# Where the big SBUF tiles begin: slots of 4096 bytes on multiples of 2 KB in a transformer block on one Trainium2 core

## The chip, the cores and the metric

The kernel runs on 1 core of one Trainium2 chip. The metric is the device time of one execution in microseconds (us), the median of several runs. A kernel's instructions stand in five queues, one for each engine: TensorE (PE; its weight loads are listed as PEld), VectorE (DVE), ScalarE (ACT), GpSimd (POOL) and SyncE (SP), which issues the DMAs.

## The reference

One transformer block on 1024 tokens of width 1024, in float32. Four mixers (banded attention, a gated recurrence, spatial gating, a gated linear recurrence) share one projection `h @ w_in`, their outputs are merged through gates, and a SwiGLU network follows:

```python
for l in range(DEPTH):                       # one layer
    h = rms_norm(x, norm_mix_pre[l])
    y = hybrid_mixer(h, w_in[l], ...)        # sum over 4 branches of sigmoid(gates) * (o_n @ w_branch), then @ w_out
    x = x + rms_norm(y, norm_mix_post[l])
    h = rms_norm(x, norm_ffn_pre[l])
    x = x + rms_norm(swiglu(h, w_ffn_in[l], w_ffn_out[l]), norm_ffn_post[l])

# of the gated linear recurrence, the causal convolution over four tokens
xp = jnp.pad(xin, ((0, 0), (CONV_W - 1, 0), (0, 0)))
xc = conv_b + xp[:, 0:S] * conv_w[0]
for j in range(1, CONV_W):
    xc = xc + xp[:, j:j + S] * conv_w[j]
```

## The kernel before, in words

**Precision.** Every float32 operand of a large product is split in two float32r parts, a high one (`split`, L133, a copy on ACT) and a low one (L134, a subtraction on DVE). A product is then three matmuls for each K tile: `mm3` (L205 to L210) multiplies high by high, high by low and low by high. Of the arguments of `nc.tensor.matmul` the one called `lhsT` is the stationary operand (128 x 128 values, loaded ahead) and the one called `rhs` is the moving operand, which is read from SBUF column by column while the matmul runs. With 512 float32 columns the moving operand is 2048 bytes long in each partition.

**Where operands lie.** SBUF is cut by pools. `slot` (L78) gives one of 33 big tiles of the pool "slots". Activations, their sums and most intermediate results lie in slots: the transposed activations `hTh`, `hTl`, `h2h`, `h2l` (two K tiles of 512 tokens in one slot), the sums `T1` to `T4`, the branches' outputs `oh`, `ol`, the fetched `back`. The pool "ring" holds the raw weight blocks (`raw`, L146) and their split parts (`whi`, `wlo`, L155 and L156). `wtmp`, `tmp` and `mtmp` give 2 KB temporaries and smaller ones from two further pools.

```python
    SW = 1028
    def slot(name, dt=F32, w=D):
        cnt[0] += 1
        t = sp.tile([P, SW], dt, tag="S", name=f"{name}_{cnt[0]}", bufs=NSLOT)
        return t[:, :w]
```

A slot is 1028 floats, 4112 bytes, and slots stand 4128 bytes apart. In the program as it is built, slot k begins at byte 27616 + 4128 k of its partition, for k = 0 to 32. Counted from a multiple of 2048, the starts are 992, 1024, 1056 and so on up to 2016: none is a multiple of 2 KB, all are multiples of 32, and every 512-column operand that lies in a slot runs across a multiple of 2 KB. The ring begins at byte 163840, which is 80 x 2048, and every one of its tiles begins on a multiple of 2 KB. The 2 KB temporaries begin 1152 bytes past one.

**Which products read which.** In the Winograd products `wino` (L320 to L357), the gates, the branch projections and the plain part of the SwiGLU input, the weights in the ring are stationary and the activations in the slots move, 512 columns at a time. In the token-major products `gemm_tm` (L224) the weights move, 256 columns at a time. In the product with `w_ffn_out` (`ffn_out`, L1168 to L1309, matmuls L1226 to L1228) both operands are split into one tile, and its second half moves, 512 columns: a ring tile as a rule, but in the last of three calls, which goes bank by bank over three pairs of K tiles (so 3 x 4 x 3 = 36 matmuls for a product), the second, fourth, sixth and seventh product take slots for it (`spare`, L1214 and L1246), since the ring alone would not hold them.

**The order.** Instructions of each engine stand in the order that the tile framework's scheduler gives, from the program's order and its priorities. The stages are: first norm and transposes; projections by Winograd, results kept in DRAM; gates ahead of time, Winograd as well; the recurrences, filled up with plain gate products; attention and spatial gating beside the gated merge; output projection and second norm; SwiGLU input by Winograd; SwiGLU output, norm, residual and store.

**The convolution.** `fetch_d` (L736) fetches the input of the linear recurrence into a slot from column 4 on, and POOL zeroes columns 0 to 3 (L738). `rglru` then reads four shifted views of 1024 columns (L747 and L749):

```python
        nc.vector.tensor_scalar(xc, X[:, 1 : S + 1], cw(0), col(C_CB + j), op0=ALU.mult, op1=ALU.add)
        for t in range(1, 4):
            nc.vector.scalar_tensor_tensor(xc, X[:, 1 + t : S + 1 + t], cw(t), xc, op0=ALU.mult, op1=ALU.add)
```

Of the kernel before, what the change touches and what calls it, by code (L numbers as in the profile page):

```python
# [17 lines left out]
P = 128  # L18
# [13 lines left out]
# columns of the packed per-partition vectors  # L32
C_GMIX, C_GFFN, C_LB, C_HG, C_GM, C_CW, C_CB, C_BA, C_BX, C_LAM = 0, 8, 16, 18, 20, 22, 30, 32, 34, 36
NCOLS = 38


@with_exitstack
def hybrid_trunk(ctx, tc, x, w_in, w_branch, w_out, w_ffn_in, w_ffn_out, cols, gpost, gfpost,
# [7 lines left out]
    cp = pool("const", 1)  # L46
    sp = pool("slots", 1)
    rp = pool("ring", 2)
    sm = pool("small", 4)
# [5 lines left out]
    def enter(name, bufs):  # L55
        """pool that gives its place to the next one"""
        if scope:
            scope.pop("s").close()
        scope["s"] = ExitStack()
        scope["p"] = scope["s"].enter_context(tc.tile_pool(name=name, bufs=bufs))  # L60
# [10 lines left out]
    # quarters of a plain gate product after each step of the recurrences, to fill the tensor engine's waits  # L71
# [3 lines left out]
    SW = 1028  # L75
    cnt = [0]

    def slot(name, dt=F32, w=D):  # L78
        cnt[0] += 1
        t = sp.tile([P, SW], dt, tag="S", name=f"{name}_{cnt[0]}", bufs=NSLOT)  # L80
        return t[:, :w]
# [44 lines left out]
    def after(ins):  # L126
        """in the program order of its engine after ins"""
        return tc.issue_after(ins.ins) if ins is not None else nullcontext()

# [20 lines left out]
    def wunit(name, src):  # L150
        """split one 4 KB unit of a raw block; src: AP of [P, a, b]"""
        cnt[0] += 1
        shp = list(src.shape)
        with tc.high_priority(AHEAD_SPLIT if started else 0):
            hi = rp.tile(shp, F32R, tag="whi", name=f"whi_{name}_{cnt[0]}", bufs=NRING)  # L155
            lo = rp.tile(shp, F32R, tag="wlo", name=f"wlo_{name}_{cnt[0]}", bufs=NRING)  # L156
            split(src, hi, lo)
        return hi, lo

    def interleave(back, front, n_back=1, n_front=1):  # L160
        """emit the two streams in turns; the longer one ends alone"""
        live = [[iter(back), n_back], [iter(front), n_front]]
        while live:
            for it in list(live):
                for _ in range(it[1]):
                    try:
                        next(it[0])
                    except StopIteration:
                        live.remove(it)
                        break  # L170

    def zipped(*streams):
        """one step of each stream in turn"""
        live = [iter(st) for st in streams]
        while live:
            for it in list(live):
                try:
                    yield next(it)
                except StopIteration:
                    live.remove(it)  # L180

    def filled(fill, stream, counts):
        """counts[i] steps of fill after the i-th step of the stream"""
        for i, _ in enumerate(stream):
            drive(take(fill, counts[i] if i < len(counts) else 0))
# [19 lines left out]
    def mm3(ps, lh, ll, rh, rl, n, more=False, ks=None):  # L205
        """accumulate over n contraction tiles; lh(k) etc. give APs; more: onto a finished group's sum"""
# [31 lines left out]
    def rstd_of(ss, n, w):  # L238
        """(ss / n + eps) ** -0.5 on [P, w]"""
        ms = small("ms", w)  # L240
        nc.gpsimd.tensor_scalar(ms, ss, 1.0 / n, EPS, op0=ALU.mult, op1=ALU.add)
        r = small("rstd", w)
        last[2] = nc.gpsimd.tensor_tensor(r, ms, neghalf[:, :w], op=ALU.pow)
        return r
# [4 lines left out]
    def halves(name):  # L249
        """token halves: slot [P, 2 k, 512] for each half and pair of k"""  # L250
# [13 lines left out]
    # Winograd's form of Strassen's product: quadrants of (columns x K) of the weights, of (K x tokens) of the  # L264
    # activations z. B_ij: K half i, token half j
    # T1 = B12 - B11, T2 = B22 - T1, T3 = B22 - B12 = T2 - B11, T4 = T2 - B21
# [40 lines left out]
    def column_sums(c0_, c1_):  # L307
        """S1 = A21 + A22, S2 = S1 - A11, S3 = A11 - A21, S4 = A12 - S2, in the order of the blocks"""
# [11 lines left out]
    def wino(ops, c0_, c1_, done):  # L320
        """two column tiles c0_, c1_ ([P, KT, P]) as the column halves of one Winograd step;
        done(column tile, token half, source, tile to use) takes the quadrants"""
# [37 lines left out]
    def normed(xtile, wait=None):  # L360
        """rms-normalised (without gain) [128 tokens, D]"""
# [8 lines left out]
    def place_T(srcs, tt, gcol, Th, Tl):  # L370
        """transpose token tiles tt, tt + 1, apply the gain per channel, split"""
# [29 lines left out]
    def twice_silu(dst, ps):  # L401
        """x * (1 + tanh(x / 2)) = 2 silu(x)"""
# [4 lines left out]
    def twice_gelu(dst, ps):  # L407
        """x * (1 + tanh(c (x + a x^3))) = 2 gelu(x)"""
# [22 lines left out]
    def fetch(key, j, w=D):  # L431
        t = slot(f"{key}{j}", w=w)
        nc.sync.dma_start(t[:, w - S :], stage[key, j])
        return t
# [3 lines left out]
    def proj_cm(key, fn, c=None):  # L438
        """fn(column tile, source, result)"""
# [17 lines left out]
    def proj_tm(key, fn):  # L457
        """token-major result, two times [P, 4 tiles, 256]"""
# [21 lines left out]
    # ======================= mixer B: gated recurrence =====================  # L480
# [27 lines left out]
    def hgrn(j):  # L508
# [5 lines left out]
        # s = t: sum over a head's channels of q k, placed on the diagonal of every tile  # L514
# [15 lines left out]
        def level(l):  # L530
            """scores of s in an even block of 2^l tokens with t in the odd block that follows"""
            # the two heads' products in turns: they lie in different row groups of the array
# [12 lines left out]
            # only the odd blocks' columns, and no rows past the last even block  # L545
# [32 lines left out]
        # state at the start of every 128-token tile  # L578
# [60 lines left out]
    # ======================= mixer A: banded attention =====================  # L639
# [93 lines left out]
    # ======================= mixer D: gated linear recurrence ==============  # L733
    Dm = {"O": [None, None]}

    def fetch_d(j):  # L736
        Dm[j] = [fetch("dx", j, w=SW), fetch("dg", j)]
        nc.gpsimd.memset(Dm[j][0][:, 0:4], 0.0)  # L738

    def rglru(j):  # L740
# [6 lines left out]
        nc.vector.tensor_scalar(xc, X[:, 1 : S + 1], cw(0), col(C_CB + j), op0=ALU.mult, op1=ALU.add)  # L747
        for t in range(1, 4):
            nc.vector.scalar_tensor_tensor(xc, X[:, 1 + t : S + 1 + t], cw(t), xc, op0=ALU.mult, op1=ALU.add)  # L749
# [12 lines left out]
        # w / 2 = 4 r softplus(-lam), a = exp(-w) = (1 - th) / (1 + th)  # L762
# [4 lines left out]
        # sqrt(1 - a^2) = 2 sqrt(th) / (1 + th)  # L767
# [15 lines left out]
    # ======================= mixer C: spatial gating =======================  # L783
# [37 lines left out]
    # ======================= gated branch merge ============================  # L821
# [5 lines left out]
    def gates_pre(items):  # L827
        """gate columns ahead of their branch: tanh kept in DRAM"""
# [68 lines left out]
    def gates_last(n, o):  # L897
        """the last branch, with the split of the result: first token half first"""
# [22 lines left out]
    # ======================= order of the mixing block =====================  # L921
# [9 lines left out]
    with tc.issue_after(last[0].ins), tc.issue_after(last[1].ins), tc.issue_after(last[2].ins):  # L931
# [24 lines left out]
        _sv = [0]  # L956

        def sv(w=2):
            _sv[0] += 1
            return cp.tile([P, w], F32, name=f"sv{_sv[0]}")  # L960

        # forget-gate lower bound: cumsum(softmax over depth) - p[0], one layer
# [13 lines left out]
        # 2 * softplus(-lam), softplus(z) = max(z, 0) + log1p(exp(-|z|))  # L976
# [26 lines left out]
    # the quadrant that no product needs waits in DRAM  # L1003
# [50 lines left out]
    # ======================= output projection, residual, second norm ======  # L1054
# [55 lines left out]
    # ======================= SwiGLU ========================================  # L1110
# [11 lines left out]
    def ffn_plain(g):  # L1122
        """hidden tiles 2 g, 2 g + 1 by direct products"""
# [18 lines left out]
        # starts on the token half that is ready first  # L1142
# [7 lines left out]
    def ffn_wino(f, rg, ru):  # L1150
        """gate and up columns of hidden tile f: the two column halves of one Winograd step"""
# [14 lines left out]
    # the same for the product of the activations with w_ffn_out: f tiles in pairs (a K half each),  # L1166
    # quadrants of (tokens x K) and of (K x columns), four PSUM banks for the 512 tokens of a product
    def ffn_out(chunk, first, final):  # L1168
# [63 lines left out]
        def prod(pst, A, B, evac, more=False, after=None):  # L1232
            """onto the four banks pst; more: onto the sum they hold"""
# [11 lines left out]
            # bank by bank  # L1245
# [20 lines left out]
        def half_done(tt, c_, second):  # L1266
            """sum of squares of a column half, then its gain; with the second half norm, residual and store"""
# [23 lines left out]
        def into_last(r, c_, second):  # L1291
            """the last product that adds to this quadrant"""
# [93 lines left out]
```

## Time and profile before

| what | value |
|---|---|
| median of 3 runs | 1629.66 us (1629.09 to 1633.43) |
| the profiled execution: span from first to last instruction | 1631.2 us |
| PE busy | 1555.7 us, 95% of the span, 7880 matmuls |
| DVE, ACT, POOL busy | 1061.5, 571.4 and 607.1 us |
| mean granted TensorE clock | 0.987 of full speed |
| DMA | 191.48 MB, mean 117 GB/s |

The page gives of the profiled execution its span alone; this lies 1.5 us above the median and within the three runs' range, so a change that is worked out from the trace is put onto the median as it stands. Matmuls are pipelined: a matmul's own duration (some 395 ns for 512 columns) spans its way through the array and overlaps the next one, so what a matmul costs is the distance from one start to the next. A window of the trace counts every matmul that reaches into it.

### The profile page before, as it was taken

How to read it: one execution, taken by the hardware profiler on the slowest of the kernel's cores; microseconds unless marked ns; L12 is line 12 of the kernel's file. 1: busy time of each engine (PE TensorE's matmuls, PEld its weight loads, DVE VectorE, ACT ScalarE, POOL GpSimd, SP SyncE). 2: the span in 40 equal slices, each digit the busy share in tenths (PEclk: the TensorE clock that was granted, in tenths of full speed). 3: DMA queues.
4: the chain of work that ended last, by engine and by line, in shares of the span. 5: the costliest groups of instructions: out<-in, count | busy, mean ns of one | idle time of the engine just before them, and what ended most of it. 6: DMA issues, size and time to landing. Idle time of an engine off the chain costs nothing. (4 is left out here: it accounts for less than half of the span.)

```text
span 1631.2 us, 20634 instructions
## 1 busy us (share of the span) xinstructions
PE 1555.7 (95%) x7880; PEld 1276.4 (78%) x7880; DVE 1061.5 (65%) x1415; ACT 571.4 (35%) x945; POOL 607.1 (37%) x477
## 2 busy tenths in 40 slices
PE   7899999999998999999999987999999999898986
PEld 7888888888887877676889966888888888686865
DVE  5985664434469475666765698555555556869898
ACT  6333332333321253324335533222222223353533
POOL 2674333322100200222332256433333334829195
PEclk9999999999999999999999998999999999999998
DMA  6234333333461148432325411222222235530212
GB/s 239 93 101 158 104 110 103 104 110 104 150 224 49 56 155 297 181 142 75 120 91 181 169 58 65 84 78 78 84 78 78 78 111 218 205 105 14 90 51 105
DMA packets 108547, 191.48 MB, mean 117 GB/s; under 512 B 6432, under 2 KB 65440, under 8 KB 108448
## 3 DMA queue, kind: packets, MB, share of 16 engines
q1 hardware_dynamic: 108448, 190.16, 33.7%
q8 instruction: 62, 1.02, 0.3%
q14 instruction: 37, 0.30, 0.1%
HBM read 136.66 MB, written 53.48 MB: 117 GB/s over the span
## 5 line engine op out<-in xcount | busy, mean ns | idle before, releaser
L134 DVE TENSOR_TENSOR wlo_ws<-s,whi_ws 128x1024 fp32r<-128x1024 f32 x78 | 120.3, 1542 | 55.1 <-ACT whi_ws L133 55.0
L354 DVE TENSOR_TENSOR u<-u,mm_w 128x512 f32<-128x512 f32 x39 | 26.8, 688 | 183.3 <-PE mm_w L210 183.3
L317 POOL TENSOR_TENSOR s<-raw_pj 128x512 f32<-128x512 f32 x38 | 64.3, 1693 | 202.2 <-DMA raw_pj<-in_w_in 194.2
L133 ACT CAST whi_ws<-s 128x1024 fp32r<-128x1024 f32 x78 | 81.9, 1050 | 162.9 <-PE mm_w L209 152.0
L1227 PE MATMUL mm_fo<-wlo_fo,whi_fo 128*128 128x512 f32 x308 | 123.2, 402 | 12.5 <-DVE wlo_fo L134 12.5
L1228 PE MATMUL mm_fo<-whi_fo,wlo_fo 128*128 128x512 f32 x308 | 119.1, 395 | 0.0
L317 POOL TENSOR_TENSOR s<-raw_fu 128x512 f32<-128x512 f32 x20 | 34.1, 1707 | 208.9 <-DMA raw_fu<-in_w_ffn_in 208.9
L1226 PE MATMUL mm_fo<-whi_fo 128*128 128x512 f32 x308 | 93.8, 397 | 9.1 <-ACT whi_fo L133 7.9
L134 DVE TENSOR_TENSOR wlo_fo<-af,whi_fo 128x512 fp32r<-128x512 f32 x66 | 72.7, 1108 | 26.9 <-ACT whi_fo L133 26.4
L1227 PEld LDWEIGHTS mm_fo<-wlo_fo,whi_fo 128*128 128x128 f32 x308 | 58.8, 191 | 31.6 <-DVE wlo_fo L134 19.3
L338 ACT COPY m<-mm_w 128x512 f32<-128x512 f32 x39 | 22.9, 586 | 161.1 <-PE mm_w L210 147.1
L133 ACT CAST whi_fo<-af 128x512 fp32r<-128x512 f32 x66 | 40.6, 622 | 108.7 <-PE mm_fo L1228 56.4
L1226 PEld LDWEIGHTS mm_fo<-whi_fo 128*128 128x128 f32 x308 | 58.6, 191 | 23.7 <-ACT whi_fo L133 9.1
L210 PE MATMUL mm_wo<-whi_wo,ml 128*128 128x256 f32 x256 | 73.2, 287 | 2.5 <-DVE ml L917 2.5
L209 PE MATMUL mm_wo<-wlo_wo,mh 128*128 128x256 f32 x256 | 73.1, 287 | 1.5 <-DVE wlo_wo L134 1.5
L208 PE MATMUL mm_w<-h2h,whi_wa 128*128 128x512 f32 x160 | 63.9, 400 | 10.3 <-ACT m L338 10.3
L208 PE MATMUL mm_wo<-whi_wo,mh 128*128 128x256 f32 x256 | 72.4, 287 | 0.9 <-ACT whi_wo L133 0.9
L1228 PEld LDWEIGHTS mm_fo<-whi_fo,wlo_fo 128*128 128x128 f32 x308 | 58.8, 191 | 12.2
L209 PE MATMUL mm_w<-h2l,whi_wa 128*128 128x512 f32 x160 | 63.5, 397 | 0.0
L210 PE MATMUL mm_w<-h2h,wlo_wa 128*128 128x512 f32 x160 | 63.5, 397 | 0.0
L208 PE MATMUL mm_w<-T2h,whi_ws 128*128 128x512 f32 x156 | 61.6, 395 | 0.7 <-ACT whi_ws L133 0.6
L208 PE MATMUL mm_w<-T4h,a 128*128 128x512 f32 x156 | 61.7, 395 | 0.0
(400 smaller groups left out, 4832.5 us busy)
## 6 DMA issues: line engine op xcount, KB each, us to landing
raw_pj<-in_w_in SPq DMA_DIRECT2D x19, 1024.0 KB, 5.8
gt<-st_g SPq DMA_DIRECT2D x22, 512.0 KB, 6.2
raw_fg<-in_w_ffn_in SPq DMA_DIRECT2D x11, 1024.0 KB, 5.0
raw_fu<-in_w_ffn_in SPq DMA_DIRECT2D x11, 1024.0 KB, 5.5
af<-act SPq DMA_DIRECT2D x22, 512.0 KB, 4.0
wf<-in_w_ffn_out SPq DMA_DIRECT2D x18, 512.0 KB, 6.0
xt<-in_x SPq DMA_DIRECT2D x16, 512.0 KB, 7.7
raw_wo<-in_w_out SPq DMA_DIRECT2D x8, 1024.0 KB, 5.2
```

Source lines behind the costliest of these rows:

```text
L133: nc.scalar.copy(hi, src)
L134: nc.vector.tensor_tensor(lo, src, hi.bitcast(F32), op=ALU.subtract)
L208: nc.tensor.matmul(ps, lhsT=lh(k), rhs=rh(k), start=(not more and k == 0), stop=False, skip_group_check=more)
L209: nc.tensor.matmul(ps, lhsT=lh(k), rhs=rl(k), start=False, stop=False, skip_group_check=more)
L210: nc.tensor.matmul(ps, lhsT=ll(k), rhs=rh(k), start=False, stop=(k == n - 1), skip_group_check=more)
L317: last_sum[0] = nc.gpsimd.tensor_tensor(out_, x0, x1_, op=op)
L338: nc.scalar.copy(m1, p1)
L354: nc.vector.tensor_tensor(u2, u2, p3, op=ALU.add)
L1226: nc.tensor.matmul(ps, lhsT=hi[:, ts], rhs=hi[:, 512:1024], start=start, stop=False, skip_group_check=more)
L1227: nc.tensor.matmul(ps, lhsT=hi[:, ts], rhs=lo[:, 512:1024], start=False, stop=False, skip_group_check=more)
L1228: nc.tensor.matmul(ps, lhsT=lo[:, ts], rhs=hi[:, 512:1024], start=False, stop=stop, skip_group_check=more)
```

## The change

The slots become 1024 floats, 4096 bytes. The pool of the small vectors moves ahead of the slots, and a filler tile of 72 floats, which nothing reads or writes, fills the space so that the first slot begins on a multiple of 2 KB. In the program as it is built, slot k now begins at byte 28672 + 4096 k, and 28672 is 14 x 2048; the ring stays at the same bytes as before, tile by tile; the 2 KB temporaries begin on multiples of 2 KB. Sixteen two-column vectors become slices of one tile (`svs`). The convolution has no room for the four zero columns any more: its input is fetched to the slot's start, the first tap covers all 1024 columns, and the other three cover 1023, 1022 and 1021 columns in place, without zeroed columns.

```diff
+FILL = 72
...
     cp = pool("const", 1)
+    sm = pool("small", 4)
+
+    fill = cp.tile([P, FILL], F32, name="fill")
     sp = pool("slots", 1)
     rp = pool("ring", 2)
-    sm = pool("small", 4)
     tp = pool("tmp", 3)
...
-    SW = 1028
     cnt = [0]
 
     def slot(name, dt=F32, w=D):
         cnt[0] += 1
-        t = sp.tile([P, SW], dt, tag="S", name=f"{name}_{cnt[0]}", bufs=NSLOT)
+        t = sp.tile([P, D], dt, tag="S", name=f"{name}_{cnt[0]}", bufs=NSLOT)
         return t[:, :w]
...
-    def fetch(key, j, w=D):
-        t = slot(f"{key}{j}", w=w)
-        nc.sync.dma_start(t[:, w - S :], stage[key, j])
+    def fetch(key, j):
+        t = slot(f"{key}{j}")
+        nc.sync.dma_start(t, stage[key, j])
         return t
...
     def fetch_d(j):
-        Dm[j] = [fetch("dx", j, w=SW), fetch("dg", j)]
-        nc.gpsimd.memset(Dm[j][0][:, 0:4], 0.0)
+        Dm[j] = [fetch("dx", j), fetch("dg", j)]
...
-        nc.vector.tensor_scalar(xc, X[:, 1 : S + 1], cw(0), col(C_CB + j), op0=ALU.mult, op1=ALU.add)
+        nc.vector.tensor_scalar(xc, X, cw(3), col(C_CB + j), op0=ALU.mult, op1=ALU.add)
         for t in range(1, 4):
-            nc.vector.scalar_tensor_tensor(xc, X[:, 1 + t : S + 1 + t], cw(t), xc, op0=ALU.mult, op1=ALU.add)
+            nc.vector.scalar_tensor_tensor(xc[:, t:], X[:, : S - t], cw(3 - t), xc[:, t:], op0=ALU.mult, op1=ALU.add)
...
         _sv = [0]
+        svs = cp.tile([P, 32], F32, name="svs")
 
         def sv(w=2):
-            _sv[0] += 1
-            return cp.tile([P, w], F32, name=f"sv{_sv[0]}")
...
+            _sv[0] += w
+            return svs[:, _sv[0] - w : _sv[0]]
```

The order of instructions stays as it is on PE, ACT and SP, row by row. The one place where rows go is POOL's queue ahead of the linear recurrence, here before the change (`dx` is the recurrence's input, `bss` and `css` are sums of squares of two mixers):

```order
L241 TENSOR_SCALAR ms_4646<-bss_4644 128x8
L243 TENSOR_TENSOR rstd_4648<-ms_4646,neghalf 128x8
L738 MEMSET dx_608_4691 128x4
L738 MEMSET dx_610_4696 128x4
L241 TENSOR_SCALAR ms_5202<-css_5197 128x2
L243 TENSOR_TENSOR rstd_5204<-ms_5202,neghalf 128x2
```

And the same place of POOL's queue with the change, where code lines are two further on:

```order
L243 TENSOR_SCALAR ms_4632<-bss_4630 128x8
L245 TENSOR_TENSOR rstd_4634<-ms_4632,neghalf 128x8
L243 TENSOR_SCALAR ms_5186<-css_5181 128x2
L245 TENSOR_TENSOR rstd_5188<-ms_5186,neghalf 128x2
```

Two zeroings have gone and nothing has moved past anything else. On DVE the convolution's rows stay in their places and get shorter, with the change:

```order
L748 TENSOR_SCALAR dxc_618_4736<-dx_608_4677,cw 128x1024
L750 SCALAR_TENSOR_TENSOR dxc_618_4736<-dx_608_4677,cw,dxc_618_4736 128x1023
L750 SCALAR_TENSOR_TENSOR dxc_618_4736<-dx_608_4677,cw,dxc_618_4736 128x1022
L748 TENSOR_SCALAR dxc_619_4747<-dx_610_4681,cw 128x1024
L750 SCALAR_TENSOR_TENSOR dxc_618_4736<-dx_608_4677,cw,dxc_618_4736 128x1021
```

So what differs for PE is no order and no wait, only the bytes at which its operands begin.

## Rows read from the trace of the kernel before

**Rows 1.** The page: span; busy us, share, instructions of each engine.

```profile
span 1631.2 us, 20634 instructions
...
PE 1555.7 (95%) x7880; PEld 1276.4 (78%) x7880; DVE 1061.5 (65%) x1415; ACT 571.4 (35%) x945; POOL 607.1 (37%) x477
```

**Rows 2.** The page: busy tenths and granted clock in 40 slices.

```profile
PE   7899999999998999999999987999999999898986
...
PEclk9999999999999999999999998999999999999998
```

**Rows 3.** Busy time by stretch, six stretches whose PE is never idle.

```profile
core 0: us, PE busy (x) PEld busy (x) DVE busy (x) ACT busy (x) POOL busy (x), PEclk, DMA share, GB/s
110.00:470.00 360.00, 360.00 (x1550) 290.75 (x1550) 186.81 (x208) 122.23 (x169) 116.34 (x76) 1.00 0.38 126
570.00:585.00 15.00, 15.00 (x66) 12.13 (x65) 11.33 (x12) 4.45 (x6) 0.00 (x0) 1.00 0.56 192
598.00:645.00 47.00, 47.00 (x204) 38.08 (x203) 30.21 (x22) 16.50 (x21) 0.00 (x0) 1.00 0.63 224
795.00:819.00 24.00, 24.00 (x105) 19.45 (x104) 20.84 (x24) 9.12 (x14) 15.35 (x11) 1.00 0.00 1
947.00:976.00 29.00, 29.00 (x126) 23.37 (x125) 28.93 (x33) 9.61 (x16) 17.27 (x11) 1.00 0.17 55
1000.00:1370.00 370.00, 370.00 (x1598) 299.69 (x1597) 197.63 (x213) 101.72 (x136) 126.89 (x76) 1.00 0.29 101
```

**Rows 4.** Busy time by stretch, two stretches of the last product (ring operands).

```profile
1420.00:1476.00 56.00, 56.00 (x248) 46.28 (x247) 41.17 (x50) 27.08 (x49) 18.06 (x12) 1.00 0.31 107
1513.00:1555.00 42.00, 42.00 (x186) 34.72 (x185) 36.03 (x57) 21.62 (x38) 8.92 (x6) 1.00 0.23 76
```

**Rows 5.** Timeline of PE at the three borders of two neighbouring products of the end.

```profile
1589.37 0.39 PE L1227 MATMUL mm_fo<-wlo_fo,whi_fo 128*128 128x512 f32 x1
...
1598.38 0.39 PE L1226 MATMUL mm_fo<-whi_fo 128*128 128x512 f32 x1
...
1606.55 0.39 PE L1227 MATMUL mm_fo<-wlo_fo,whi_fo 128*128 128x512 f32 x1
```

**Rows 6.** Groups of PE by form: first and last of 13 on L208, 512 columns.

```profile
L208 PE MATMUL mm_w<-h2h,whi_wa 128*128 128x512 f32 x160 | 63.9, 400 | 10.3 <-ACT m L338 10.3
...
L208 PE MATMUL mm_fu<-h2h,whi_fu 128*128 128x512 f32 x32 | 12.6, 395 | 0.0
```

**Rows 7.** Busy time by stretch, two mixed stretches of the mixers and the gates.

```profile
480.00:570.00 90.00, 84.97 (x781) 73.16 (x781) 67.47 (x142) 17.11 (x32) 9.40 (x12) 1.00 0.21 68
645.00:795.00 150.00, 149.71 (x778) 110.53 (x777) 94.55 (x230) 52.63 (x124) 40.61 (x71) 1.00 0.43 155
```

**Rows 8.** The four longest of PE's waits: who waited, us, times, longest.

```profile
PE mm_fo L1227 <- DVE wlo_fo L134: 12.5, 15, 4.4
PE mm_w L208 <- ACT m L338: 11.0, 2, 10.3
PE mx_tr L377 <- DVE xn L367: 10.3, 3, 7.6
PE mm_fo L1226 <- ACT whi_fo L133: 7.9, 3, 3.9
```

**Rows 9.** ACT and DVE, L133 and L134: slot source, then ring source, min/median/max ns.

```profile
L133 ACT CAST whi_ws<-s x78: 1032/1050/1060, 101.6 to 1360.3; 128x1024 fp32r<-128x1024 f32 x78
...
L133 ACT CAST whi_wo<-raw_wo x16: 1030/1051/1057, 796.8 to 909.9; 128x1024 fp32r<-128x1024 f32 x16
...
L134 DVE TENSOR_TENSOR wlo_ws<-s,whi_ws x78: 1212/1227/2329, 102.6 to 1361.4; 128x1024 fp32r<-128x1024 f32 x78
...
L134 DVE TENSOR_TENSOR wlo_wo<-raw_wo,whi_wo x16: 1211/1226/2309, 800.1 to 911.0; 128x1024 fp32r<-128x1024 f32 x16
```

**Rows 10.** POOL's zeroing of the first four columns, and DVE's taps of the convolution.

```profile
L738 POOL MEMSET dx<- x2: 101/102/102, 566.3 to 566.3; 128x4 f32 x2
...
L749 DVE SCALAR_TENSOR_TENSOR dxc<-dx,cw,dxc x6: 1279/1282/1285, 578.1 to 586.2; 128x1024 f32<-128x1024 f32 x6
```

## The prediction

> **What bounds the kernel now.** I read the page first. [...] Then I asked for the busy time of each engine by stretch. In six stretches, 845 us together, PE is never idle, the clock is 1.00, and DVE, ACT and POOL have room in the two long ones: 187 and 198 us of DVE in 360 and 370 us [rows 3]. In these stretches the end is set by how fast PE starts one matmul after the other, which I call the pitch. A window also counts a matmul that began up to 0.39 us before it, so the pitch is (window + 0.39 us) / count.
>
> For the six stretches, whose matmuls all move 512 columns out of slots, this gives (845 + 6 x 0.39) / 3649 = 232.2 ns; the two long ones alone give 360.39 / 1550 = 232.5 ns and 370.39 / 1598 = 231.8 ns [rows 3]. For two busy stretches of the last product, whose moving operands lie in the ring, it is 56.39 / 248 = 227.4 ns and 42.39 / 186 = 227.9 ns, together 227.6 ns [rows 4]. All of these are float32r matmuls of the same size, each with its own weight load, at the same clock. The ring's operands begin on a multiple of 2 KB and fill exactly 2 KB; a slot's operand before the change never does, and always runs across such a multiple.
>
> The stages differ in more than that, so I looked for a pair that does not. In the final call of `ffn_out` the fourth product takes slots and the fifth the ring; both go bank by bank onto the same four PSUM banks, one right after the other. From the start at 1589.37 to the one at 1598.38 there are 39 matmuls (35 of the fourth product and 4 of the sixth, which takes slots too): 9.01 us / 39 = 231.0 ns. From 1598.38 to 1606.55 there are the fifth product's 36: 8.17 us / 36 = 226.9 ns [rows 5]. With the place of the moving operand the pitch moves by 4.1 ns, in one and the same stage.
>
> **The change part by part.** *Matmuls that move 512 columns out of slots.* Line 208 has 13 such forms, from 160 down to 32 instructions, 1444 together [rows 6]; lines 209 and 210 have the same counts, so 3 x 1444 = 4332. After the change each reads 2 KB that begin on a multiple of 2 KB, as a ring operand does. How PE then runs is not in the trace for these stages; the nearest rows bound it. The least gain per matmul that I see reason for is 2.6 ns, from the fastest slot-fed row to the ring: I take 230.0 ns for the first, 1 ns under the 231.0 ns of [rows 5] as its uncertainty, against 227.4 ns [rows 4]. The most is 232.5 ns [rows 3] to 226.9 ns [rows 5], 5.6 ns. I take the long stretches against the ring's, 232.2 - 227.6 = 4.6 ns, because they average over hundreds of matmuls beside other engines' work.
>
> In the six stretches there are 3649 - 6 x 1.7 = 3639 matmuls (0.39 us over the pitch makes 1.7 counted too many in each window). PE has no idle time there, so all of it reaches the end: 3639 x 4.6 ns = 16.7 us. The other 4332 - 3639 = 693 lie in mixed stretches. There PE is busy 85.0 of 90 us and 149.7 of 150 us [rows 7], but some of that waits on the recurrences' DVE chain, and the small matmuls in between are unknown to me; I count half, 693 x 2.3 = 1.6 us. The final call's four slot-fed products are 4 x 36 = 144 matmuls at 4.1 ns, 0.6 us, of which I count 0.4 us, since DVE and POOL end that stage. Sum: 16.7 + 1.6 + 0.4 = 18.7 us.
>
> [...]
>
> *Stationary operands and narrow matmuls.* The token-major products move 256 columns out of the ring, which stays; only their stationary operands lie in slots. Weight loads run beside the matmuls (1276 us busy against 1556 [rows 1]); I count nothing, for the loads have that cover. Bounds: a tenth of the 4.6 ns, up or down, on all the other 7880 - 4332 - 924 = 2624 matmuls (924 are the last product's), 1.2 us either way.
>
> *Work on DVE, ACT and POOL.* A copy of 1024 columns out of a slot takes 1050 ns on ACT and one out of the ring 1051; the subtraction on DVE takes 1227 and 1226 ns [rows 9]. So no duration there should move, and where PE is busy throughout, it would be hidden anyway.
>
> *DMAs.* All transfers keep their sizes and their place in SP's queue. No DMA is among PE's longest waits [rows 8], so a transfer that lands sooner or later by a fraction of a us is covered by the work that PE holds; if the cover were gone, the first load of x would be the place, ahead of PE's longest wait on the norm, 7.6 us [rows 8]. I count nothing.
>
> *Convolution.* Two zeroings of 102 ns go from POOL, and six taps of 1282 ns lose 1, 2 or 3 columns of 1024, some 2 ns each [rows 10]; they lie at 566 to 586 us beside a PE that is busy [rows 3]. Nothing. What follows them in POOL's queue, two small operations of the norm, may start 0.2 us sooner, which nobody waits for.
>
> *What comes next.* Where PE gets 2% faster, the results that it waits for must come 2% sooner: DVE is busy half of the long stretches and POOL a third [rows 3], so I expect no new wait there.
>
> The sum is against the profiled execution, 1631.2 us, and gives 1612.5 us; that execution is 0.1% above the median of the runs, and on the median it is 1629.7 - 18.7 = 1611 us.
>
> **The rivals.**
> *A part of it only (8%).* The slots' pitch falls by the least gain, because the weights' or the accumulation's place has a share in the 4.6 ns, or DVE's chain takes back the rest. 4476 x 2.6 ns = 11.6 us, so 1618 us. For it speaks that the pair of [rows 5] shows 4.1 and not 4.6 ns; against it that PE has no idle time in 845 us.
> *Addresses cost nothing (6%).* The 4.6 ns would belong to the stage, and the pair of [rows 5] would be chance. Then nothing changes: 1629.7 us, and the two long stretches keep 232 ns. [...] Against it stands the step at 1598.38 us, within 36 matmuls.
> *Equal starts collide: slower (2%).* Now all slots begin at the same place of a 4 KB period, the ring's parts and the 2 KB temporaries at the same place of a 2 KB period. If PE's reading of an operand is held up by DVE's, ACT's or POOL's access to the same place of another tile, the long stretches pay, where DVE writes the ring's parts and POOL the sums. It decides from the point at which it costs more than the 4.6 ns gained, that is a pitch over 232.2 ns; at 2 ns more it is 4332 x 2 = 8.7 us, 1638 us. Against it: in the ring-fed stretches, whose operands already begin alike, the pitch is 227.9 ns with DVE busy for 36 of 42 us and 227.4 ns with 41 of 56 [rows 4], so half a ns at most.
> That the change does not do what it says I leave out: the built program's addresses are multiples of 2 KB.
>
> **How the numbers follow.** The forecast has 84%, the three rivals 8, 6 and 2%. The time is the forecast's, 1611 us. Its lower end is the largest gain on all slot-fed matmuls, 4476 x 5.6 ns = 25 us, so 1604.6, and I write 1604. The upper end takes in the partial rival, 1618, with 2 us for the spread of the runs: 1620. About 0.3% (4.9 us) is what a measurement of this kernel can tell from no change; forecast and partial rival are beyond it, so faster has 92%, same 6% and slower 2%.
>
> **What would show it.** Right: the matmul counts stay, PE's share stays near 95%, the stretch of the first Winograd products (before at 110 to 470 us) shows about 1581 instead of 1550 matmuls in 360 us, 228 ns each; the fourth and fifth product of the final call have one pitch; ACT and DVE keep 1050 and 1227 ns. The end of the second long stretch, before at 1370 us, comes some 18 us sooner, and the tail behind it keeps its length. Wrong: a pitch still at 232 ns (addresses cost nothing), a pitch that is higher beside DVE's work than without (collision), or a pitch of 228 ns with new waits of PE on DVE or ACT (the gain given back).

## The result, and the profile after

The change takes 1611.83 us (median of 4 runs, 1611.13 to 1613.24) against 1630.18 us for the kernel before (4 runs, 1629.09 to 1633.43): a ratio of 0.9888, 95% interval 0.9874 to 0.9902. It is faster by 18.4 us between the medians; 18.7 us had been worked out, for 1611 us.

The page after, the lines that answer to [rows 1, 2]:

```profile
span 1609.9 us, 20631 instructions
...
PE 1535.5 (95%) x7880; PEld 1278.8 (79%) x7880; DVE 1059.6 (66%) x1415; ACT 571.7 (36%) x945; POOL 607.1 (38%) x475
...
PE   7899999999998999999999988999999999898986
...
PEclk9999999999999999999999998999999999999988
```

The same 7880 matmuls, the same share of 95%, but 20.2 us less of PE's busy time. DVE, ACT and POOL are as busy as before; POOL has lost its two zeroings. The two long stretches, whose ends now come 8 and 22 us sooner, and a ring-fed one, with the columns of [rows 3]:

```profile
110.00:462.00 352.00, 352.00 (x1555) 291.52 (x1554) 186.38 (x208) 122.88 (x170) 117.28 (x76) 1.00 0.39 129
...
985.00:1348.00 363.00, 363.00 (x1603) 300.66 (x1603) 197.91 (x214) 101.83 (x136) 129.37 (x77) 1.00 0.30 103
1400.00:1450.00 50.00, 50.00 (x222) 41.42 (x221) 34.61 (x45) 25.30 (x46) 12.95 (x8) 1.00 0.34 116
```

By the prediction's rule the pitch is 352.39 / 1555 = 226.6 ns, 363.39 / 1603 = 226.7 ns and 50.39 / 222 = 227.0 ns: slot-fed and ring-fed matmuls now have one pitch. The two long ones together stood at 730.78 / 3148 = 232.1 ns [rows 3] and stand at 715.78 / 3158 = 226.7 ns: a gain of 5.5 ns for each matmul, where 4.6 had been forecast. Where along the program this adds up is read from first and last starts (us) of PE's matmuls by tile, before:

```profile
L208 PE MATMUL mm_proj<-oh,whi_wb x128: 387/396/582, 643.0 to 818.4; 128*128 128x512 f32 x128
L208 PE MATMUL mm_fu<-h2h,whi_fu x32: 389/396/400, 928.0 to 973.1; 128*128 128x512 f32 x32
L208 PE MATMUL mm_w<-h2h,whi_wa x160: 389/395/795, 973.8 to 1364.2; 128*128 128x512 f32 x160
L1226 PE MATMUL mm_fo<-whi_fo x308: 388/389/632, 1373.2 to 1617.3; 128*128 128x512 f32 x154
```

and after:

```profile
L210 PE MATMUL mm_proj<-oh,whi_wb x128: 387/393/583, 632.5 to 806.7; 128*128 128x512 f32 x128
L210 PE MATMUL mm_fu<-h2h,whi_fu x32: 389/389/396, 913.6 to 958.9; 128*128 128x512 f32 x32
L210 PE MATMUL mm_w<-h2h,whi_wa x160: 389/389/796, 959.5 to 1342.3; 128*128 128x512 f32 x160
L1228 PE MATMUL mm_fo<-whi_fo x308: 388/389/796, 1351.1 to 1596.0; 128*128 128x512 f32 x154
```

The gain is 10.5 us at the first branch projection, 14.4 us at the first product of the SwiGLU input, 21.9 us at that Winograd's end, and 21.3 us at the last matmul: it grows where slots are read, and the tail gives back 0.6 us. PE's longest waits are those of [rows 8], none of them new:

```profile
PE mm_fo L1229 <- DVE wlo_fo L136: 12.1, 14, 4.4
PE mm_w L210 <- ACT m L340: 11.8, 2, 10.9
PE mx_tr L379 <- DVE xn L369: 10.5, 3, 7.5
```

The border of two products in the final call, the rows that answer to [rows 5], in PE's timeline after:

```profile
1568.28 0.40 PE L1229 MATMUL mm_fo<-wlo_fo,whi_fo 128*128 128x512 f32 x1
...
1577.14 0.39 PE L1228 MATMUL mm_fo<-whi_fo 128*128 128x512 f32 x1
...
1585.30 0.39 PE L1229 MATMUL mm_fo<-wlo_fo,whi_fo 128*128 128x512 f32 x1
```

The 39 matmuls of slots take 8.86 us, 227.2 ns each (231.0 before), the 36 of the ring 8.16 us, 226.7 ns: one pitch, as forecast. And the other engines' rows that answer to [rows 9, 10], ACT, then DVE:

```profile
L135 ACT CAST whi_ws<-s x78: 1034/1054/1058, 101.6 to 1338.5; 128x1024 fp32r<-128x1024 f32 x78
...
L136 DVE TENSOR_TENSOR wlo_ws<-s,whi_ws x78: 1211/1226/2373, 102.7 to 1339.6; 128x1024 fp32r<-128x1024 f32 x78
...
L750 DVE SCALAR_TENSOR_TENSOR dxc<-dx,cw,dxc x6: 1274/1280/1284, 567.9 to 575.9; 128x1023 f32<-128x1023 f32 x2, 128x1022 f32<-128x1022 f32 x2, 128x1021 f32<-128x1021 f32 x2
```

Of all these rows only PE's pitch has moved.

### The profile page after: what moved, and what is told of

Read it like the earlier page. It is cut to its first block, busy times and chain, and to the rows that moved or that the text cites. A ratio compares the mean times of both kernels' runs of the same rounds, so it can differ in the third digit from the quotient of the medians.

```text
span 1609.9 us, 20631 instructions
## 1 busy us (share of the span) xinstructions
PE 1535.5 (95%) x7880; PEld 1278.8 (79%) x7880; DVE 1059.6 (66%) x1415; ACT 571.7 (36%) x945; POOL 607.1 (38%) x475
## 5 line engine op out<-in xcount | busy, mean ns | idle before, releaser
L319 POOL TENSOR_TENSOR s<-raw_pj 128x512 f32<-128x512 f32 x38 | 59.0, 1553 | 197.2 <-DMA raw_pj<-in_w_in 187.1
L1229 PEld LDWEIGHTS mm_fo<-wlo_fo,whi_fo 128*128 128x128 f32 x308 | 59.4, 193 | 30.7 <-DVE wlo_fo L136 18.4
```

The source lines that it names most:

```text
L319: last_sum[0] = nc.gpsimd.tensor_tensor(out_, x0, x1_, op=op)
L1229: nc.tensor.matmul(ps, lhsT=hi[:, ts], rhs=lo[:, 512:1024], start=False, stop=False, skip_group_check=more)
```

## The experiments

What stayed open was the reason. The theory on record was that an operand is slower when it runs across a multiple of 2 KB. A rival: what counts is how the moving and the stationary operand begin relative to each other. A third: the other parts of the change (convolution, vectors) bring some of the gain. In the diffs `FILL` is the filler ahead of the slots, and `pad` a tile between two pools that nothing reads or writes; together they move one pool and leave the others.

**Slots off a multiple of 2 KB, and the ring off the slots.** The kernel before, unchanged, is `e0`. The next two begin the slots 32 and 256 bytes short of a multiple of 2 KB, with the ring where it was; the fourth leaves the slots and moves ring and temporaries by 512 bytes. (The grain, in the expectations below, is the multiple on which starts would have to lie.)

```diff
e1   -FILL = 72   +FILL = 64   +pad = pool("pad", 1).tile([P, 8], F32, name="pad")
e2   -FILL = 72   +FILL = 8    +pad = pool("pad", 1).tile([P, 64], F32, name="pad")
e3                             +pad = pool("pad", 1).tile([P, 128], F32, name="pad")
```

> The kernel before, unchanged, profiled a second time. All theories: the pitch (window + 0.39 us over count) of the stretches 110 to 470 us and 1000 to 1370 us stays at 232 ns. What it decides is whether the first profile's span of 1631.2 us is typical: if its executions scatter by a few us, the span comes out at 1628 to 1630 us, and the 3 us must lie outside the two long stretches.

> The changed kernel, with every slot 32 bytes earlier (2016 past a multiple of 2 KB, 4096 apart) and ring and temporaries where the change has them. Theory of straddling (a 512-column operand that runs across a multiple of 2 KB costs PE some 5.5 ns more): all 4332 + 144 slot-fed matmuls are slow again, pitch 231 to 233 ns in the long stretches, 1629 to 1633 us. Theory of the slots' spacing (4128 against 4096 bytes apart is what matters, since operands read together then begin at different places): the spacing stays at 4096, so 226.6 ns and 1612 us. Theory of the temporaries (their alignment brought the gain): 226.6 ns and 1612 us.

> The same with every slot 256 bytes earlier (1792 past a multiple of 2 KB): each begins on a multiple of 256, and each 512-column operand still straddles a multiple of 2 KB. Theory of straddling: 231 to 233 ns, 1629 to 1633 us. Rival, alignment of the start (any start on a multiple of 64, 128 or 256 bytes is as good): 226.6 ns and 1612 us. A value between, near 229 ns and 1620 us, would say that both have a share.

> The changed kernel, with slots as the change has them and the ring and all temporaries 512 bytes later. Theory of straddling: the Winograd stretches keep 226.6 ns, for their moving operands lie in slots; the ring-fed matmuls of the last product, 780, go from 227 to 231 to 232 ns, at most 780 x 5 ns = 3.9 us, less where DVE or POOL end that stage; of the 256-column matmuls, which move 1 KB out of the ring, every second one straddles a multiple of 2 KB and should get slower by some ns, at most 672 x 5 ns = 3.4 us: 1613 to 1618 us. If instead a multiple of 1 KB were what counts, every 256-column matmul would get slower. Theory of alignment to 512 bytes or less: nothing moves, 1612 us. Theory that temporaries matter: the Winograd stretches get slower, toward 232 ns.

Measured, against 1628.83 us for the kernel before: `e0` 1633.17 us in its one run, with x1551 and x1598 in the two long stretches; `e1` 1634.45 us, ratio 1.0032 (1.0021 to 1.0044); `e2` 1610.31 us, 0.9883 (0.9869 to 0.9898); `e3` 1610.23 us, 0.9883 (0.9867 to 0.9900). PE's busy time by stretch (us, count, then clock, DMA share, GB/s), `e1`:

```profile
110.00:470.00 360.00, 360.00 (x1544) 1.00 0.38 125
1000.00:1370.00 370.00, 370.00 (x1588) 1.00 0.30 102
```

`e2`, whose every slot-fed operand of 512 columns crosses a multiple of 2 KB:

```profile
110.00:462.00 352.00, 352.00 (x1555) 1.00 0.39 130
985.00:1348.00 363.00, 363.00 (x1603) 1.00 0.29 101
```

and `e3`:

```profile
110.00:462.00 352.00, 352.00 (x1555) 1.00 0.39 129
985.00:1348.00 363.00, 363.00 (x1604) 1.00 0.30 103
```

`e1` has 730.78 / 3132 = 233.3 ns, `e2` 715.78 / 3158 = 226.7 ns. So crossing a 2 KB border costs nothing, and my stated reason fell; 32 bytes cost 6.6 ns, 256 and 512 bytes nothing.

**Which distance, and which of the two.** 64 and 128 bytes between slots and ring; then the slots left on 2 KB and ring and temporaries 32 bytes late; then everything 32 bytes late, so that nothing begins on 2 KB but all begin alike.

```diff
e4   -FILL = 72   +FILL = 56   +pad = pool("pad", 1).tile([P, 16], F32, name="pad")
e5   -FILL = 72   +FILL = 40   +pad = pool("pad", 1).tile([P, 32], F32, name="pad")
e6                             +pad = pool("pad", 1).tile([P, 8], F32, name="pad")
e7   -FILL = 72   +FILL = 80
```

> The changed kernel with every slot 64 bytes earlier (1984 past a multiple of 2 KB), ring and temporaries where the change has them. Straddling has fallen with the slots 256 bytes early, so what is left is a grain G between 64 and 256 bytes on which operands must begin. If G is 64: 226.6 ns in the long stretches and 1610 to 1613 us. If G is 128 or 256: 232 to 234 ns and 1630 to 1636 us, as with 32 bytes. From the kernel before, whose slots on multiples of 64 were no faster when three followed each other, I expect G over 64, without being sure.

> The same with every slot 128 bytes earlier (1920 past a multiple of 2 KB). If G is 64 or 128: 226.6 ns and 1610 to 1613 us. If G is 256: 232 to 234 ns and 1630 to 1636 us. Something between would say that the cost grows with the distance from the grain.

> The changed kernel with slots on multiples of 2 KB, and ring and temporaries 32 bytes later. In the Winograd products the moving operand then begins on the grain and the stationary one off it. Theory of the moving operand alone: the Winograd stretches keep 226.6 ns, the ring-fed matmuls of the last product go from 227 to 231 to 233 ns, the 256-column ones get slower, 1612 to 1618 us. Theory that moving and stationary must lie alike: 232 to 234 ns in the Winograd stretches, 1630 us or more. Theory of two terms with opposite signs (a moving operand off the grain costs some 6.5 ns, a stationary one off it gives back some 3 ns, as the 256-column matmuls ran at 117 ns with slots 32 bytes early and at 120 ns with the change): 223 to 224 ns in the Winograd stretches, 4332 x 3 = 13 us less there, some 780 x 3.5 and 1344 x 5 ns more elsewhere: 1602 to 1610 us.

> The changed kernel with all big tiles, slots, ring and temporaries alike, 32 bytes later: nothing changes in where they lie to each other, and none begins on the grain. Theory that moving and stationary must lie alike: 226.6 ns, 120 ns for 256 columns and 1610 to 1613 us. Theory of the moving operand alone: 232 to 234 ns for every 512-column matmul, the last product's too, and over 1630 us. Theory of two terms: 6.5 - 3 = 3.5 ns more, 230 ns, 1626 to 1630 us.

Measured, against 1631.07 us: `e4` 1636.56 us, 1.0031 (1.0019 to 1.0043); `e5` 1631.12 us, 1.0000 (0.9991 to 1.0010); `e6` 1633.83 us, 1.0017 (1.0008 to 1.0027); `e7` 1610.25 us, 0.9873 (0.9858 to 0.9888). PE by stretch in `e6`, the slots on 2 KB (the third row is a ring-fed stretch):

```profile
110.00:470.00 360.00, 360.00 (x1545) 1.00 0.37 125
1000.00:1370.00 370.00, 370.00 (x1587) 1.00 0.29 100
1420.00:1476.00 56.00, 56.00 (x248) 1.00 0.33 113
```

and in `e7`, nothing on 2 KB:

```profile
110.00:462.00 352.00, 352.00 (x1554) 1.00 0.39 130
985.00:1348.00 363.00, 363.00 (x1603) 1.00 0.30 103
```

This pair decides. `e6` keeps the slots, from which the Winograd products move, at the change's bytes and runs at 730.78 / 3132 = 233.3 ns; `e7` moves them off and runs at 715.78 / 3157 = 226.7 ns. So 32 bytes more in the absolute address cost nothing; what counts is that moving and stationary operands begin alike, and by the distances tried (32, 64, 128 against 0, 256, 512 bytes) alike means modulo 256 bytes. `e4` and `e5` have the pitch of `e1` (x1545 and x1544 in the first stretch, x1588 in both in the second). That `e4`'s runs lie 5 us above `e5`'s is not seen in these stretches; behind 1370 us `e4`'s profiled execution was granted a clock of 0.94 and `e5`'s 0.96. These two executions took 1634.20 and 1633.36 us, so the traces show little of the 5 us. Whether addresses have a part in that stays open.

How far this goes can be read from the kernel before, whose slots begin 32 bytes apart modulo 256, so that some operands are alike by chance. With the starts of single matmuls in its trace and the addresses in the built program, 334 of the 3146 matmuls of the two long stretches that are followed by another at once have a moving and a stationary operand that begin alike. The next one starts 232.4 ns after them on average, and 232.1 ns after all 3146. A single alike matmul among unlike ones gains nothing; fast were streams in which the operands of all matmuls begin alike.

**Only one kind of product apart.** The ring stays with the slots, and only the pool of the 2 KB temporaries begins 32 bytes late. The split weights that the Winograd products multiply with `T4` (the trace lists them as `a`) lie there, stationary: 3 x 156 = 468 matmuls.

```diff
e8   +pad2 = pool("pad2", 1).tile([P, 8], F32, name="pad2")
```

> The changed kernel with the 2 KB temporaries alone 32 bytes later; slots and ring lie as the change has them. Of the matmuls, the temporaries feed only the stationary operand of the fourth Winograd sum (a22 with T4): 12 of 84 in each Winograd step, 468 in all. Theory that the moving operand and the stationary one of a matmul must begin alike modulo 256 bytes: these 468 go from 226.7 to 233 ns and the rest stays, so a long stretch has a pitch of 226.7 + 6.5/7 = 227.6 ns and the time is 468 x 6.5 ns = 3 us more than the change's, 1613 to 1615 us. Theory that the moving operands have to lie alike among themselves and the stationary ones do not matter: 226.7 ns everywhere and 1610 to 1612 us. If one unlike operand throws its neighbours out too: more than 3 us.

Measured: 1616.01 us against 1629.45 us, ratio 0.9921 (0.9904 to 0.9937), 5.2 us more than the change beside it in the same series (`e11`, 1610.79 us). PE's timeline of `e8` shows what one block does, every line the first of a group of matmuls:

```profile
205.00 0.39 PE L211 MATMUL mm_w<-T1h,whi_ws 128*128 128x512 f32 x1
...
207.72 0.39 PE L211 MATMUL mm_w<-T4h,a 128*128 128x512 f32 x1
207.95 0.40 PE L211 MATMUL mm_w<-T3h,whi_ws 128*128 128x512 f32 x1
...
210.69 0.39 PE L212 MATMUL mm_w<-T4l,a 128*128 128x512 f32 x1
...
213.25 0.39 PE L211 MATMUL mm_w<-hTh,whi_wa 128*128 128x512 f32 x1
...
216.00 0.39 PE L211 MATMUL mm_w<-T2h,whi_ws 128*128 128x512 f32 x1
```

The 12 matmuls from 205.00 us take 226.7 ns each, the 12 of `T3` from 207.95 us 228.3 ns, the 11 of `T4` with their displaced weights 2.56 us / 11 = 232.7 ns, and the 12 after them, whose operands are alike again, 2.75 us / 12 = 229.2 ns. So the effect sits with the products that are apart, and their neighbours pay some of it as well: 468 x 6 ns is 2.8 us of the 5.2. The matmul just ahead pays too: at the 68 places in the trace where a displaced stationary operand follows an alike one without another product size between them, the displaced matmul starts 235 ns after the one before it, and 227 ns in the change (medians).

**The rest of the change alone.** The kernel before with the new convolution, without zeroing, and with the vectors in one tile (wide enough that every other tile keeps its byte).

```diff
-        Dm[j] = [fetch("dx", j, w=SW), fetch("dg", j)]
-        nc.gpsimd.memset(Dm[j][0][:, 0:4], 0.0)
+        Dm[j] = [fetch("dx", j), fetch("dg", j)]
...
+        svs = cp.tile([P, 128], F32, name="svs")
```

> The kernel before with the other parts of the change alone: the convolution without zeroed columns and the small vectors in one tile (held at the size that they had, so that every big tile begins where it did). All theories that lay the gain to where operands begin: 232 ns in the long stretches and the time of the kernel before, within 1 us. If the convolution or the waits that it drops had a share: less by that share.

Measured: 1628.66 us against 1629.45 us, ratio 0.9996 (0.9987 to 1.0006). It brings nothing that can be measured (the interval reaches from 2 us less to 1 us more); the first long stretch has x1551 in 360 us as in `e0`. The gain is the addresses'.

**The narrow matmuls.** In the token-major products 256 columns move out of the ring against a slot. There the sign turns: in a stretch of the output projection that is nothing else, the change is slower than `e1`. So in `e10` the ring's tiles of split weights are 256 bytes larger, and the token-major units alone begin 32 bytes late in them; `e11` is the change itself beside it.

```diff
-            hi = rp.tile(shp, F32R, tag="whi", ...)
+            hi = rp.tile([P, 1088], F32R, tag="whi", ...)
...
+            hi, lo = (t[:, off : off + 1024].rearrange("p (a b) -> p a b", b=shp[2]) for t in (hi, lo))
...
-            return [wunit(name, raw[:, 0:4, :]), wunit(name, raw[:, 4:8, :])]
+            return [wunit(name, raw[:, 0:4, :], 8), wunit(name, raw[:, 4:8, :], 8)]
```

> A try at a faster kernel: the change, with the split weights of the token-major products 32 bytes off in their ring tiles (tiles of 4352 bytes, 17 x 256; the output of the squares, which nobody reads, is made bfloat16 for the space). The 1344 matmuls that move 256 columns then begin unlike their stationary operands, the 512-column ones alike. With slots 32 bytes early the 256-column matmuls ran at 117 ns, with the change at 120. If that holds here: 117 ns, and at most 1344 x 3 ns = 4 us less than the change, more likely 2 to 3 us, since the first stage and the second norm wait for other engines: ratio to the kernel before 0.986 against the change's 0.988. If the 117 ns came from something else: 120 ns and the change's time.

> The change itself, on the same chip as the three others, to compare them with: ratio 0.987 to 0.989 to the kernel before, 226.7 ns in the long stretches, 120 ns for 256 columns.

Measured, against 1629.45 us: `e10` 1609.10 us, 0.9879 (0.9864 to 0.9894); `e11` 1610.79 us, 0.9887 (0.9872 to 0.9902). PE in 44 us of the output projection in which 256-column matmuls are all that PE does, before, after, `e1` and `e10`:

```profile
840.00:884.00 44.00, 44.00 (x374) 1.00 0.42 144
```

```profile
826.00:870.00 44.00, 44.00 (x369) 1.00 0.45 156
```

```profile
839.00:883.00 44.00, 44.00 (x379) 1.00 0.45 158
```

```profile
826.00:870.00 44.00, 44.00 (x379) 1.00 0.45 159
```

With 0.28 us for matmuls that reach into the window, that is 44.28 us over the count: 118.4 ns before, 120.0 ns after, 116.8 ns in `e1` and in `e10`. Narrow matmuls are faster apart, by 3.2 ns at 32 bytes; the same window from 839 us has x375 in `e4` and x373 in `e5`, 118.1 ns at 64 bytes and 118.7 ns at 128. Over the 3 x 256 + 9 x 64 = 1344 matmuls of the token-major products 3.2 ns would be 4.3 us. Between `e11` and `e10` the medians differ by 1.7 us and the intervals overlap: the shorter pitch is shown, a gain in time is not.

## Why the prediction was right, and where it was not

**Right.** The bound (PE's pitch in stretches without idle time), the pair of [rows 5] as the sign that the place of an operand sets that pitch, the other engines' durations, the DMAs, the waits, and the time. Of the signs named, the first Winograd stretch went past its mark: 1555 matmuls in 352 us, 1590 in 360, where 1581 had been worked out from 228 ns.

**The reason was wrong.** The step said that a ring operand "begin[s] on a multiple of 2 KB and fill[s] exactly 2 KB", and a slot's runs across such a multiple. `e2`, `e3` and `e7` run across it, or move one side off it, and keep the whole gain (226.7, 226.6 and 226.7 ns); `e6` keeps the slots on 2 KB and loses it (233.3 ns). What the change did was to give slots the same start as the ring, modulo 256 bytes. In the ring-fed rows that served as the model both operands lie in ring tiles, and so begin alike wherever the ring is: in `e6` they keep their pitch, 56.39 / 248 = 227.4 ns from 1420 to 1476 us. In the slow half of [rows 5] operands shared a tile as well: of the final call's slot-fed matmuls that another follows at once, 70 of 126 have operands that begin alike, yet they took 230.5 ns. There the starts differ from one matmul to the next, in the ring they don't. So the forecast transferred a right number for a wrong reason; with a ring at another start it would have failed, as `e6` shows.

**The main term was too small.** 4.6 ns for each matmul; measured 5.5 ns. The model rows [rows 4] gave 227.6 ns, but slots reach 226.7 ns, the value of the ring-fed half of [rows 5]. 3639 x 5.5 ns is 20.0 us instead of 16.7 us; followed from matmul to matmul, the six stretches of [rows 3] fall by 19.7 us. The mixed stretches of [rows 7] brought 0.9 us, where 1.6 us had been counted.

**Narrow matmuls were costed at nothing.** They got 1.6 ns slower, 1344 x 1.6 ns = 2.2 us on the other side, nearly twice the 1.2 us kept as a bound; the sign of a tenth of the wide ones' gain was not known, and `e10` shows why: for them, being alike is the bad case (120.0 ns in the change, 116.8 ns 32 bytes apart).

**The base.** The span falls by 21.3 us, the medians by 18.4. `e0`'s span of 1631.1 us belongs to a time of 1633.17 us, so the execution whose trace was read was one of the longer ones: by the same difference its 1631.2 us are a time of some 1633.3 us, 3.6 us above the median of 1629.66 and not 1.5. One execution differs from the next by several us at the same pitch: `e9`, with the addresses of before, has a span of 1627.1 us, and against it the change's span falls by 17.2 us. Most of the 4.1 us between these two executions lies in the output projection, where the granted clock of before falls below 1.00: PE before

```profile
820.00:840.00 20.00, 16.86 (x126) 0.91 0.32 107
...
880.00:900.00 20.00, 18.22 (x146) 0.95 0.60 213
900.00:920.00 20.00, 20.00 (x168) 0.97 0.55 203
```

and PE in `e9`

```profile
820.00:840.00 20.00, 17.60 (x146) 1.00 0.35 123
880.00:900.00 20.00, 18.22 (x154) 1.00 0.59 208
900.00:920.00 20.00, 20.00 (x164) 1.00 0.37 137
```

From its first matmul to its last (the tile `mm_wo`) that projection takes 103.2 us before (819.1 to 922.3), 99.5 us in `e9` (818.1 to 917.6) and 100.8 us after (807.3 to 908.1): 2.4 us of the 21.3 us arise there, and against the same addresses at a clock of 1.00 the change is 1.3 us slower, about what its 768 narrow matmuls cost at 1.6 ns each. Over the whole execution the mean granted clock is no better with the change, 0.986 against 0.987.

**How near the number came.** That 18.7 us lie so close to the 18.4 us between the medians is in part luck: the main term was 3.0 us too small, and what set that off were terms too large or missing on the other side, the narrow matmuls' 2.2 us, 0.7 us in the mixed stretches and the final call's 0.4 us, where the tail gave back 0.6 us instead.

**The rivals.** A part only: fell, the gain for each matmul was above the forecast. Addresses cost nothing: fell, by the ratio and by `e1` (233.3 ns) against `e2` (226.7 ns), one kernel with 224 bytes between them. In both every operand of these matmuls begins on a multiple of 32 bytes, and the slots of `e1`, 32 bytes off the ring, cost 6.6 ns for each matmul. Equal starts collide: not seen for wide operands, `e7` and the change are as fast with all starts alike (226.7 ns in both); for narrow ones something of that sign exists (120.0 ns alike, 116.8 ns apart), which is not shown to come from another engine.

## What to carry to other kernels

Where PE never waits, measure its pitch (window over count) per product and compare products of one shape: 2% between them (here 232.1 against 226.7 ns) was a property of the operands that no busy share showed, 95% before and after. Then try the SBUF starts of the moving and the stationary operand alike modulo 256 bytes where 512 float32r columns move (226.7 ns in these runs, against 233.3 ns at 32 bytes apart), for all matmuls of a stream and not for single ones (232.4 ns after one that was alike, in the kernel before); where 256 columns move, 32 bytes apart was the faster (116.8 against 120.0 ns). `e7` needed no absolute alignment (226.7 ns with nothing on 2 KB), and a test that shifts both sides together tells the one from the other. Before a row is used as the model for another, ask in what else it differs: here the fast rows had no 2 KB border inside an operand, but also one start for all their operands modulo 256 bytes.

## What was not expected of the hardware

- Two operands' starts matter relative to each other: 226.7 ns alike against 233.3 ns apart for 512 columns, and the other way for 256 columns, 120.0 against 116.8 ns. Both directions in one kernel, at a granted clock of 1.00.
- A product whose operands are apart slows the matmuls around it too (`e8`: 235 ns from the start of the one ahead to the start of the first displaced one, 227 ns in the change; 229.2 ns in the 12 that follow, against 226.7 ns).
- Why it is so stays open. Traffic of other engines is an unlikely reason: in `e8` the pitch changes with the product, from 226.7 to 232.7 ns and back within some 10 us, but none of the runs moves PE's operands without moving what other engines read and write.
- In the kernel before, where starts differ by multiples of 32 bytes from one matmul to the next, the pitch lies between the two, at 232.1 ns, and single alike matmuls gain nothing (232.4 ns). How many neighbours must be alike, and whether the moving operands must be alike among themselves, was not tried apart.
